# Layer norms of a network's first block: the features centred early on the mean of their first half, the variance corrected at the end

## The chip, the cores and the metric

The kernel runs on one core of one Trainium2 chip. The metric is the time of one execution on the device in microseconds (us), in fp32 accuracy, with all weights read from HBM. Five engines work beside one another, each in its own order: PE multiplies matrices, DVE and ACT work on rows of elements (DVE with two inputs, ACT with a function per element, for some of which it first loads a table), POOL has little to do here, and SP issues nearly all DMAs, in order, on one queue.

## The reference

The network has a first block of four layers (a gated convolution, a state space model "ssm", an rwkv mixer, a second convolution) and after it two blocks of attention and feed forward layers on two streams. The change concerns what closes each of the four layers:

```
for i in range(4):
    y = mixer_i(x)                                   # conv, ssm, rwkv, conv
    r = 8**0.25 * x + y
    r = r + (p[i] @ ple_proj[i]) * sigmoid(r @ ple_gate[i])
    mu = r.mean(-1); var = square(r - mu).mean(-1)
    x = (r - mu) * rsqrt(var + 1e-5) * ln_g[i] + ln_b[i]
```

`x` holds 256 tokens of 1024 features.

## The kernel before, in words

Features lie on partitions and tokens along the free axis, so `x` and `r` are 8 chunks (NCH) of 128 features by 256 tokens (S). A sum over features is then a matmul: the constant matrix `mean`, 128 x 128 with 1/1024 everywhere, times a chunk gives that chunk's part of the mean, the same on all partitions.

Weights come as fp32 tiles `w` of 128 x 1024 from HBM. Most are split into `whi` (ACT, L601) and `wlo` (DVE, L602), the operand likewise into `rs_hi`, `rs_lo`, and each product of 128 x 128 by 128 x 256 is three matmuls; a tile of `ple_gate` is 24 matmuls. The weights `ssm_in` are not split: their tile is 8 fp32 matmuls, straight from `w`. The sums `ps_st` are fp32 matmuls too. Each fp32 matmul leaves two records in the trace.

A stage of the first block ends in `finish`, which writes `r` and its split, and `ple_norm` follows. It runs `ple_proj` (its result is `pp`) and then the 8 tiles of `ple_gate`, one chunk m of the output per tile. For each, `take` runs: ACT a tanh out of PSUM (`ta<-ps_mm`), DVE `ta<-ta,pp`, DVE `r<-ta,r`, and for m = 1 to 6 DVE `total<-total,r`. After the last tile PE sums `total` and `r[7]` to the mean (`ps_st<-total`, `ps_st<-r`), DVE subtracts it from each chunk (`r<-r,ps_st`), ACT squares each (`sq<-r`), DVE adds up the squares (`sq<-sq`), PE sums them with three fp32 matmuls (`ps_st<-sq`). `rsqrt` is Ln, Exp and Square on ACT and two DVE steps, all under the name `tc`. Then DVE multiplies each chunk by `rstd` (`r<-r,pr,tc`, 8 of them) and ACT adds the bias (`x<-r,pr`); the next stage's matmuls read `x`. L403 and L433 are the lines of the helpers that record an operation of ACT or DVE, and a matmul.

The ssm stage that follows the first of the layer norms multiplies `x` by 16 tiles of `ssm_in` and treats the 8 chunks of its state one after another; chunk by chunk these are called A0, B1, A2, B3 up to B7 here, since two sets of buffers alternate. One chunk takes trigonometric functions on ACT, two wide multiplications, two additions, 8 scans and two more wide multiplications on DVE (`ssm_m`), then a sum on PE and `y`.

What fills gaps: from the start of the kernel a side generator `ada` makes the modulation vectors of the later blocks. It loads 512 KB tiles of `ada` through the same ring of four weight buffers `w` and the same SP queue, and DVE reduces each tile twice (`junk<-w,cond`, L1360). `Net.weave` steps it whenever the planned clock of the kernel has passed its due time and `hold` is zero; `ple_norm` raises `hold` when tile 6 of `ple_gate` has been taken and lowers it at its end. From the rwkv stage on the second stream's matmuls are woven in as well, which they are not before. The planner's model of the engines (`Model`, `Engine`, `TensorE`) with the pauses that a stage asks for (`yield 1.5`, `yield 3.5`) decides when a generator goes on; a scheduler behind it sets the order of the instructions on each engine.

Of the kernel before, what the change touches and what calls it, by code (L numbers as in the profile page):

```python
# [13 lines left out]
AF = mybir.ActivationFunctionType  # L14
ALU = mybir.AluOpType
# [3 lines left out]
D = 1024  # L19
S = 256  # L20
NCH = D // 128
# [65 lines left out]
def constants():  # L87
    groups = {}
    c = groups["base"] = Cols()
    c.add("ident", np.eye(128))  # L90
    c.add("mean", np.full((128, 128), 1.0 / D))
    c = groups["ssm"] = Cols()
    c.add("tshift", np.broadcast_to(np.arange(S // 2) - S // 4, (128, S // 2)))
    c.add("bd32", np.kron(np.eye(4), np.ones((32, 32))))
    c = groups["base"]
    bd = np.kron(np.eye(2), np.ones((64, 64)))
    c.add("bdmean", bd / 64)
    c = groups["rwkv"] = Cols()

    s_, t_ = np.arange(64)[:, None], np.arange(64)[None, :]  # L100
    strict, incl = (s_ < t_) * 1.0, (s_ <= t_) * 1.0
    c.add("p1mask", np.block([[strict, incl], [strict, incl]]))
    two = lambda m: np.kron(np.eye(2), m)
    c.add("ltmask", two(strict.T))
    c.add("eye", np.tile(np.eye(64), (2, 1)))
    for lv in range(6):
        b = 1 << lv
        m = (s_ // (2 * b) == t_ // (2 * b)) & (s_ // b % 2 == 0) & (t_ // b % 2 == 1)
        c.add(f"lv{lv}", np.tile(m * 1.0, (2, 1)))
    c.add("lvT0", two(((s_ == t_ + 1) & (s_ % 2 == 1)) * 1.0))  # L110
    c = groups["rwkv"]
    c.add("restart", np.broadcast_to((np.arange(S) % 64 != 0) * 1.0, (128, S)))
    c = groups["second"] = Cols()
    b96 = np.zeros((128, 128))
    b96[:96, :96] = 1.0 / 96
    c.add("b96", b96)
    ca, sa, ra = rope_head(64)
    cb, sb, rb = rope_head(32)
    c.add("cos_a", np.tile(ca.T, (2, 1)))
    c.add("sin_a", np.tile(sa.T, (2, 1)))  # L120
    c.add("rot_a", np.kron(np.eye(2), ra))
    full = lambda v, fill: np.concatenate([np.full((64, S), fill), v.T, np.full((32, S), fill)])
    c.add("cos_b", full(cb, 1.0))
    c.add("sin_b", full(sb, 0.0))
    r = np.zeros((128, 128))
    r[64:96, 64:96] = rb
    c.add("rot_b", r)
    t = np.arange(128)
    for lv in range(7):
        b = 1 << lv  # L130
        c.add(f"hg{lv}", (t[:, None] // (2 * b) == t[None, :] // (2 * b)) & (t[:, None] // b != t[None, :] // b))
    return groups


def rope_head(dim):

    f32 = np.float32
    t = np.arange(S)

    def one(pos, d):  # L140
        inv = np.power(f32(10000.0), -np.arange(0, d, 2, dtype=f32) / f32(d)).astype(f32)
        ang = pos.astype(f32)[:, None] * inv[None, :]
        ang = np.concatenate([ang, ang], axis=-1)
        return np.cos(ang), np.sin(ang)

    cr, sr = one(t // 64, dim // 2)
    cc, sc = one(t % 64, dim // 2)
    q = dim // 4
    m = np.zeros((dim, dim))
    for h in range(2):  # L150
        for i in range(q):
            a, b = h * 2 * q + i, h * 2 * q + q + i
            m[b, a], m[a, b] = -1.0, 1.0
    return np.concatenate([cr, cc], -1), np.concatenate([sr, sc], -1), m


def pack(inp):
# [97 lines left out]
    for g, c in constants().items():  # L255
        o["const_" + g] = c.array()
        cat.update({n: (g, k) for n, k in c.at.items()})
# [182 lines left out]
class Net:  # L440
# [339 lines left out]
    def ple_norm(self, R, i, split=True, free=2):  # L780

        nc = self.nc
        r, rs = R
        pp = yield from self.ple_proj(i)
        total = self.slot(free, [S], "total")

        def take(m, ps):
            t = self.tmp("ta")
            self.act(t, ps, AF.Tanh, scale=0.5)
            self.V.scalar_tensor_tensor(out=t, in0=t, scalar=1.0, in1=pp[:, m], op0=ALU.add, op1=ALU.mult)  # L790
            self.V.scalar_tensor_tensor(out=r[:, m], in0=t, scalar=0.5, in1=r[:, m], op0=ALU.mult, op1=ALU.add)
            if m == NCH - 2:
                self.hold += 1
            if 0 < m < NCH - 1:
                self.V.tensor_tensor(out=total, in0=total if m > 1 else r[:, 0], in1=r[:, m], op=ALU.add)

        yield from self.linear(f"ple_gate{i}", rs or r, take)
        yield 1.5
        mean = self.bsum(self.c("mean"), lambda k: (total, r[:, NCH - 1])[k], 2)
        sq = self.slot(2, [NCH, S], "sq")  # L800
        for k in range(NCH):
            self.V.tensor_tensor(out=r[:, k], in0=r[:, k], in1=mean, op=ALU.subtract)
            self.A.activation(out=sq[:, k], in_=r[:, k], func=AF.Square)
            if k > 2:
                self.V.tensor_tensor(out=sq[:, 0], in0=sq[:, 0], in1=sq[:, k - 2], op=ALU.add)
        yield 3.5
        var = self.bsum(self.c("mean"), lambda k: sq[:, (0, NCH - 2, NCH - 1)[k]], 3)
        rstd = self.rsqrt(var, 1e-5)
        x = self.xp.tile([128, NCH, S], F32, name="x")
        xs = self.pair(0, 1, "xs") if split else None  # L810
        for k in range(NCH):
            self.V.scalar_tensor_tensor(out=r[:, k], in0=r[:, k], scalar=self.p("ln_g", i * NCH + k), in1=rstd, op0=ALU.mult, op1=ALU.mult)
            self.A.activation(out=x[:, k], in_=r[:, k], func=AF.Identity, bias=self.p("ln_b", i * NCH + k))
            if split:
                self.split(x[:, k], xs[0][:, k], xs[1][:, k])
        self.hold -= 1
        yield 6.0
        return x, xs
# [1134 lines left out]
```

## Time and profile before

| what | value |
|---|---|
| time, median of 3 runs | 2898.12 us |
| lowest, highest | 2895.41, 2901.14 us |
| the profiled execution, its own time | 2892.28 us |
| its span | 2890.5 us |
| busy: PE, DVE, ACT | 2749.0, 2129.7, 1613.4 us |

The span is the time from the first to the last record on the core; 1.8 us of the profiled execution lie around it. The four layer norms follow one another at about 175, 396, 846 and 1020 us of the span, and the ssm stage takes the time from 195 to 323 us. A row of a timeline gives start, length, engine, line, operation, output and inputs; "x4" is four instructions in a row, and the bracket at its end says how long the engine was idle before and which engine's result ended that.

### The profile page before, as it was taken

The numbers are of one execution on the slowest core, as the hardware profiler recorded it, in microseconds if no ns is written. First come the engines' busy times: TensorE is split into PE (matmuls) and PEld (weight loads), VectorE is DVE, ScalarE is ACT, GpSimd is POOL, SyncE is SP. The second block draws the span as 40 slices with busy tenths as digits, with TensorE's granted clock in tenths as the row PEclk, the third lists the DMA queues.
The fourth block names the chain that finished last, engine by engine and source line by source line (L and its number), as shares of the span: only waits on it lengthen the run. The fifth ranks groups of instructions, "written<-read, shape, count | busy, mean of one in ns | idle before, by whom it ended". The sixth has DMA issues, their size and how long they took to land.

```text
span 2890.5 us, 58487 instructions
## 1 busy us (share of the span) xinstructions
PE 2749.0 (95%) x23798; PEld 2601.8 (90%) x23798; DVE 2129.7 (74%) x3950; ACT 1613.4 (56%) x2982; POOL 14.8 (1%) x41
## 2 busy tenths in 40 slices
PE   8978879899999999999999999999999999999999
PEld 8967779678999999898998978999999999996999
DVE  8868977566778798898899887877854336676655
ACT  5543657666664465877576766545423234466443
POOL 0000000000000000000000000000000000000000
PEclk9989889999999999999999999999999999999999
DMA  7643536001557657565575644666534223222554
GB/s 270 207 143 113 172 102 192 14 24 64 195 168 240 223 181 236 185 215 183 193 236 160 198 146 148 216 223 202 179 128 139 92 82 98 88 88 65 162 182 140
DMA packets 129295, 454.94 MB, mean 157 GB/s; under 512 B 14336, under 2 KB 18688, under 8 KB 128384
## 3 DMA queue, kind: packets, MB, share of 16 engines
q1 hardware_dynamic: 129024, 451.19, 48.3%
q8 instruction: 187, 3.06, 0.4%
q14 instruction: 84, 0.69, 0.1%
HBM read 450.09 MB, written 1.05 MB: 156 GB/s over the span
## 4 chain that ended last, share of the span: by engine, by line
PE 72%; DVE 13%; ACT 7%; DMA 5%; issue 3%; SPq 0%; ACTq 0%; DVEq 0%
PE ps_mm L433 62%; PE ps_ca L433 5%; DMA w<-in_ada_dram 4%; DVE wlo L602 3%; DVE junk L1360 3%; PE ps_cb L433 2%; DVE ssm_m L403 2%; ACT whi L601 2%; PE ps_st L433 2%; DVE tc L403 1%; PE ps_cb L437 1%; ACT L403 1%; ACT rw_b L403 1%; ACT tc L403 1%; DVE h_lo L403 1%
## 5 line engine op out<-in xcount | busy, mean ns | idle before, releaser
L601 ACT ACTIVATE whi<-w 128x1024 fp32r<-128x1024 f32 (+1 forms) x687 | 715.6, 1043 | 736.3 <-PE ps_mm L433 489.6
L602 DVE TENSOR_TENSOR wlo<-w,whi 128x1024 fp32r<-128x1024 f32 (+1 forms) x687 | 824.5, 1202 | 239.6 <-ACT whi L601 237.6
L433 PE MATMUL ps_mm<-h_hi,whi 128*128 128x256 f32 x3024 | 867.9, 289 | 6.4 <-ACT h_hi L403 4.8
L433 PE MATMUL ps_mm<-h_lo,whi 128*128 128x256 f32 x3024 | 856.5, 284 | 2.0 <-DVE h_lo L403 1.9
L433 PE MATMUL ps_mm<-h_hi,wlo 128*128 128x256 f32 x3024 | 853.0, 283 | 2.4 <-DVE wlo L602 2.4
L433 PEld LDWEIGHTS ps_mm<-h_hi,whi 128*128 128x128 f32 x3024 | 570.1, 189 | 15.8 <-ACT h_hi L403 6.5
L433 PEld LDWEIGHTS ps_mm<-h_lo,whi 128*128 128x128 f32 x3024 | 569.8, 189 | 8.3 <-DVE h_lo L403 3.2
L433 PEld LDWEIGHTS ps_mm<-h_hi,wlo 128*128 128x128 f32 x3024 | 571.2, 189 | 6.4 <-DVE wlo L602 4.0
L1360 DVE SCALAR_TENSOR_TENSOR junk<-w,cond 128x1024 bf16<-128x1024 f32 x288 | 351.0, 1219 | 123.9 <-DMA w<-in_ada_dram 122.8
L433 PE MATMUL ps_mm<-d_hi,whi 128*128 128x256 f32 x1232 | 352.9, 287 | 0.9 <-ACT d_hi L403 0.9
L433 PE MATMUL ps_mm<-d_hi,wlo 128*128 128x256 f32 x1232 | 348.5, 283 | 3.7 <-DVE wlo L602 3.6
L433 PE MATMUL ps_mm<-d_lo,whi 128*128 128x256 f32 x1232 | 349.9, 284 | 0.0
L433 PEld LDWEIGHTS ps_mm<-d_hi,wlo 128*128 128x128 f32 x1232 | 233.2, 189 | 4.9 <-DVE wlo L602 4.7
L433 PEld LDWEIGHTS ps_mm<-d_hi,whi 128*128 128x128 f32 x1232 | 232.6, 189 | 3.6 <-issue 2.0
L433 PEld LDWEIGHTS ps_mm<-d_lo,whi 128*128 128x128 f32 x1232 | 232.1, 188 | 2.7 <-issue 1.6
L403 DVE TENSOR_TENSOR td<-td,ps_mm 128x256 f32<-128x256 f32 x154 | 64.1, 416 | 82.5 <-PE ps_mm L433 79.1
L403 ACT ACT_TABLE_LOAD x84 | 107.8, 1283 | 2.5 <-PEq L1944 0.7
L403 ACT ACTIVATE d_hi<-td 128x256 fp32r<-128x256 f32 x154 | 63.0, 409 | 74.5 <-DVE td L403 73.8
L433 PE MATMUL ps_mm<-x_hi,whi 128*128 128x256 f32 x256 | 73.3, 287 | 11.8 <-ACT whi L601 11.8
L403 ACT ACTIVATE tc<-tc 128x256 f32<-128x256 f32 x182 | 75.1, 413 | 5.6 <-DVE tc L403 2.8
L403 ACT ACTIVATE td<-ps_mm 128x256 f32<-128x256 f32 x154 | 57.1, 372 | 33.1 <-PE ps_mm L433 32.6
L433 PE MATMUL ps_mm<-xs_hi,whi 128*128 128x256 f32 x256 | 72.7, 284 | 1.6 <-ACT whi L601 1.6
(465 smaller groups left out, 5287.9 us busy)
## 6 DMA issues: line engine op xcount, KB each, us to landing
w<-in_ffn_in_dram SPq DMA_DIRECT2D x268, 512.0 KB, 4.1
w<-in_ada_dram SPq DMA_DIRECT2D x144, 512.0 KB, 4.4
w<-in_ffn_out_dram SPq DMA_DIRECT2D x96, 512.0 KB, 4.0
w<-in_conv_in_dram SPq DMA_DIRECT2D x64, 512.0 KB, 4.6
w<-in_ffn_out_dram SPq DMA_DIRECT2D x48, 384.0 KB, 3.5
w<-in_ab_in_dram SPq DMA_DIRECT2D x34, 512.0 KB, 4.4
w<-in_ple_gate_dram SPq DMA_DIRECT2D x32, 512.0 KB, 4.4
w<-in_conv_out_dram SPq DMA_DIRECT2D x16, 512.0 KB, 4.7
```

The source lines that it names most:

```text
L403: return f(**kw)
L433: self.t.matmul(out, lhsT=lhsT, rhs=rhs, start=start, stop=stop)
L437: self.t.transpose(out, in_, ident)
L601: nc.scalar.activation(out=hi[:, :n], in_=w[:, :n], func=AF.Copy)
L602: nc.vector.tensor_tensor(out=lo[:, :n], in0=w[:, :n], in1=hi[:, :n].bitcast(F32), op=ALU.subtract)
L1360: nc.vector.scalar_tensor_tensor(out=self.junk, in0=w, scalar=1.0, in1=cb[:, s], op0=ALU.mult, op1=ALU.mult, accum_out=m[:, t, s:s + 1])
```

## The change

A constant `mean4`, 2/1024 everywhere, joins `mean`. `total` becomes a temporary `te` and adds only the chunks 0 to 3. As soon as chunk 4 is taken, one matmul of `mean4` with it gives c, the mean of the first half (`ps_ca<-te`). Chunks are then centred on c (`r<-r,ps_ca`), squared and added up while the tiles 5 to 7 are still multiplied. At the end four matmuls sum the centred chunks 4 to 7, whose result is the mean that remains, and two sum the squares; DVE takes the square of the remaining mean from the variance (`te<-ps_st,te`) and subtracts the remaining mean from all eight chunks (`r<-r,ps_st`) before they are multiplied by `rstd`. `hold` rises when chunk 4 is taken, the pause after the tiles is 1.0 and the second pause is gone. In the third layer norm the squares lie in another slot than before.

```diff
@@ -89,6 +89,7 @@
     c = groups["base"] = Cols()
     c.add("ident", np.eye(128))
     c.add("mean", np.full((128, 128), 1.0 / D))
+    c.add("mean4", np.full((128, 128), 2.0 / D))
     c = groups["ssm"] = Cols()
     c.add("tshift", np.broadcast_to(np.arange(S // 2) - S // 4, (128, S // 2)))
     c.add("bd32", np.kron(np.eye(4), np.ones((32, 32))))
@@ -782,30 +783,52 @@
         nc = self.nc
         r, rs = R
         pp = yield from self.ple_proj(i)
-        total = self.slot(free, [S], "total")
+        V, A, T = self.V, self.A, self.T
+        tt = lambda o, a, b, op: V.tensor_tensor(out=o, in0=a, in1=b, op=op)
+
+
+        H = NCH // 2
+        ss = self.slot(free, [NCH, S], "sq")
+        total = self.tmp("te")
+        st = {}
+
+        def centre(k):
+            tt(r[:, k], r[:, k], st["c"], ALU.subtract)
+            A.activation(out=ss[:, k], in_=r[:, k], func=AF.Square)
+            if 0 < k < NCH - 1:
+                tt(ss[:, 0], ss[:, 0], ss[:, k], ALU.add)
 
         def take(m, ps):
             t = self.tmp("ta")
             self.act(t, ps, AF.Tanh, scale=0.5)
-            self.V.scalar_tensor_tensor(out=t, in0=t, scalar=1.0, in1=pp[:, m], op0=ALU.add, op1=ALU.mult)
-            self.V.scalar_tensor_tensor(out=r[:, m], in0=t, scalar=0.5, in1=r[:, m], op0=ALU.mult, op1=ALU.add)
-            if m == NCH - 2:
+            V.scalar_tensor_tensor(out=t, in0=t, scalar=1.0, in1=pp[:, m], op0=ALU.add, op1=ALU.mult)
+            V.scalar_tensor_tensor(out=r[:, m], in0=t, scalar=0.5, in1=r[:, m], op0=ALU.mult, op1=ALU.add)
+            if m == H:
                 self.hold += 1
-            if 0 < m < NCH - 1:
-                self.V.tensor_tensor(out=total, in0=total if m > 1 else r[:, 0], in1=r[:, m], op=ALU.add)
+            if 0 < m < H:
+                tt(total, total if m > 1 else r[:, 0], r[:, m], ALU.add)
+            if m == H:
+                st["c"] = self.ps("ca")[:, :S]
+                T.matmul(st["c"], lhsT=self.c("mean4"), rhs=total, start=True, stop=True)
+                for k in range(3):
+                    centre(k)
+            elif m > H:
+                for k in ((), (3, 4), (5,), (6,))[m - H] if m < NCH - 1 else (6, 7):
+                    centre(k)
 
         yield from self.linear(f"ple_gate{i}", rs or r, take)
-        yield 1.5
-        mean = self.bsum(self.c("mean"), lambda k: (total, r[:, NCH - 1])[k], 2)
-        sq = self.slot(2, [NCH, S], "sq")
+        yield 1.0
+        ps = self.ps("st")
+        mean, var = ps[:, :S], ps[:, S:]
+        for k in range(H, NCH):
+            T.matmul(mean, lhsT=self.c("mean"), rhs=r[:, k], start=k == H, stop=k == NCH - 1)
+        for k in (0, NCH - 1):
+            T.matmul(var, lhsT=self.c("mean"), rhs=ss[:, k], start=k == 0, stop=k > 0)
+        A.activation(out=total, in_=mean, func=AF.Square)
+        tt(total, var, total, ALU.subtract)
+        rstd = self.rsqrt(total, 1e-5)
         for k in range(NCH):
-            self.V.tensor_tensor(out=r[:, k], in0=r[:, k], in1=mean, op=ALU.subtract)
-            self.A.activation(out=sq[:, k], in_=r[:, k], func=AF.Square)
-            if k > 2:
-                self.V.tensor_tensor(out=sq[:, 0], in0=sq[:, 0], in1=sq[:, k - 2], op=ALU.add)
-        yield 3.5
-        var = self.bsum(self.c("mean"), lambda k: sq[:, (0, NCH - 2, NCH - 1)[k]], 3)
-        rstd = self.rsqrt(var, 1e-5)
+            tt(r[:, k], r[:, k], mean, ALU.subtract)
         x = self.xp.tile([128, NCH, S], F32, name="x")
         xs = self.pair(0, 1, "xs") if split else None
         for k in range(NCH):
```

DVE in the middle of the first layer norm. Before, from the result of chunk 4 on, with `ada`'s reductions between:

```order
L403 TENSOR_TENSOR total<-total,r 128x256
L403 SCALAR_TENSOR_TENSOR r<-ta,r 128x256
L1360 SCALAR_TENSOR_TENSOR junk,mod<-w,cond_157 128x1024
L403 TENSOR_TENSOR total<-total,r 128x256
L1360 SCALAR_TENSOR_TENSOR junk,mod<-w,cond_157 128x1024
L403 SCALAR_TENSOR_TENSOR ta<-ta,pp 128x256
L1360 SCALAR_TENSOR_TENSOR junk,mod<-w,cond_157 128x1024
L403 SCALAR_TENSOR_TENSOR r<-ta,r 128x256
L1360 SCALAR_TENSOR_TENSOR junk,mod<-w,cond_157 128x1024
```

And after the change:

```order
L404 TENSOR_TENSOR te<-te,r 128x256
L404 SCALAR_TENSOR_TENSOR r<-ta,r 128x256
L1383 SCALAR_TENSOR_TENSOR junk,mod<-w,cond_157 128x1024
L404 TENSOR_TENSOR r<-r,ps_ca 128x256 x3
L404 SCALAR_TENSOR_TENSOR ta<-ta,pp 128x256
L404 TENSOR_TENSOR sq<-sq 128x256
L404 SCALAR_TENSOR_TENSOR r<-ta,r 128x256
L404 TENSOR_TENSOR sq<-sq 128x256
L404 TENSOR_TENSOR r<-r,ps_ca 128x256 x3
L404 TENSOR_TENSOR sq<-sq 128x256
L404 SCALAR_TENSOR_TENSOR ta<-ta,pp 128x256
```

In place of `ada`'s reductions and `total` there stand subtractions of c and sums of squares. The matmul that makes c stands in PE's order behind 14 of the 24 matmuls of tile 5 and waits for `te` of chunk 3, the row ahead of the last `r` here.

PE and DVE from the end of the first layer norm to the start of the ssm stage. PE before:

```order
L433 MATMUL ps_mm<-rs_hi,wlo 128x256
L433 MATMUL ps_st<-total,cs_base 128x256
L433 MATMUL ps_st<-r,cs_base 128x256
L433 MATMUL ps_st<-sq,cs_base 128x256 x3
L433 MATMUL ps_mm<-x,w 128x256 x24
L433 MATMUL ps_ca<-ta,bT_206 128x128
```

PE after:

```order
L434 MATMUL ps_mm<-rs_hi,wlo 128x256
L434 MATMUL ps_st<-r,cs_base 128x256 x4
L434 MATMUL ps_st<-sq,cs_base 128x256 x2
L434 MATMUL ps_mm<-x,w 128x256 x12
L434 MATMUL ps_ca<-ta,bT_206 128x128
```

The sums ask for four matmuls of `r` and two of `sq` in place of one of `total`, one of `r` and three of `sq`, and the first group of the ssm state (`ps_ca<-ta`) stands behind 12 matmuls with `x`, no longer behind 24. DVE before:

```order
L403 SCALAR_TENSOR_TENSOR ssm_m_2152<-ssm_m_2152 128x512
L1360 SCALAR_TENSOR_TENSOR junk,mod<-w,cond_157 128x1024 x3
L403 SCALAR_TENSOR_TENSOR tc<-ps_st,tc 128x256
L1360 SCALAR_TENSOR_TENSOR junk,mod<-w,cond_157 128x1024
L403 SCALAR_TENSOR_TENSOR tc<-tc 128x256
L1360 SCALAR_TENSOR_TENSOR junk,mod<-w,cond_157 128x1024
L403 SCALAR_TENSOR_TENSOR r<-r,pr,tc 128x256 x8
L403 TENSOR_TENSOR ssm_m_2152<-ssm_m_2153 128x1024 x2
L403 TENSOR_TENSOR ssm_m_2153<-ssm_m_2152 128x4x128 x2
L403 SCALAR_TENSOR_TENSOR ssm_m_2153<-rho,ssm_m_2153 128x128 x8
L403 TENSOR_TENSOR ssm_m_2152<-ssm_m_2153 128x1024 x2
L403 TENSOR_TENSOR ssm_m_2154<-ssm_m_2155 128x1024 x2
```

DVE after:

```order
L404 TENSOR_TENSOR te<-ps_st,te 128x256
L404 TENSOR_TENSOR r<-r,ps_st 128x256 x8
L1383 SCALAR_TENSOR_TENSOR junk,mod<-w,cond_157 128x1024
L404 SCALAR_TENSOR_TENSOR tc<-te,tc 128x256
L404 SCALAR_TENSOR_TENSOR tc<-tc 128x256
L404 SCALAR_TENSOR_TENSOR r<-r,pr,tc 128x256 x8
L1383 SCALAR_TENSOR_TENSOR junk,mod<-w,cond_157 128x1024 x2
L404 TENSOR_TENSOR ssm_m_2158<-ssm_m_2159 128x1024 x2
L404 TENSOR_TENSOR ssm_m_2159<-ssm_m_2158 128x4x128 x2
L404 SCALAR_TENSOR_TENSOR ssm_m_2159<-rho,ssm_m_2159 128x128 x8
L404 TENSOR_TENSOR ssm_m_2158<-ssm_m_2159 128x1024 x2
L404 SCALAR_TENSOR_TENSOR y<-u,pr,ps_st 128x2x128
```

Fewer reductions of `ada` stand between the steps of `rsqrt`, and two of them stand ahead of the first multiplication of A0. After A0 the chain goes on to `y`; before, B1's multiplications followed, so that the ssm stage had four rounds of two chunks, (A0,B1) to (A6,B7), and now has A0 alone, three pairs (B1,A2), (B3,A4), (B5,A6), and B7 alone.

SP's queue at the same place, before (the names carry their buffers' numbers):

```order
L596 DMA w_2156<-in_ssm_in_dram 128x1024
L1357 DMA w_2168<-in_ada0_dram 128x1024
L1357 DMA w_2172<-in_ada0_dram 128x1024
L596 DMA w_2176<-in_ssm_in_dram 128x1024
L1357 DMA w_2199<-in_ada0_dram 128x1024
L596 DMA w_2203<-in_ssm_in_dram 128x1024
```

And after:

```order
L1380 DMA w_2174<-in_ada0_dram 128x1024
L1380 DMA w_2178<-in_ada0_dram 128x1024
L597 DMA w_2182<-in_ssm_in_dram 128x1024
L597 DMA w_2243<-in_ssm_in_dram 128x1024
L597 DMA w_2266<-in_ssm_in_dram 128x1024
L775 DMA te_3715<-in_pT_dram 128x256
L1380 DMA w_2278<-in_ada0_dram 128x1024
L597 DMA w_2282<-in_ssm_in_dram 128x1024
L597 DMA w_2381<-in_ssm_in_dram 128x1024
```

`w_2278` is the `ada` tile of the two reductions ahead of A0. Its transfer waits for PE, that is, until the first tile of `ssm_in` (`w_2162`, before `w_2156`) has been multiplied and its buffer is free; the `ada` tiles at this place before (`w_2168` to `w_2226`) wait for DVE alone.

## Rows read from the trace of the kernel before

**Rows 1.** The page's part 1: busy time of each engine, its share, its instructions

```profile
PE 2749.0 (95%) x23798; PEld 2601.8 (90%) x23798; DVE 2129.7 (74%) x3950; ACT 1613.4 (56%) x2982; POOL 14.8 (1%) x41
```

**Rows 2.** Windows over three layer norms: stretch, its length, busy time by engine, PEclk, DMA

```profile
168.00:196.00 28.00, 8.35 (x33) 6.08 (x32) 22.92 (x51) 16.28 (x29) 0.00 (x0) 0.59 0.34 104
392.00:425.00 33.00, 20.76 (x112) 17.32 (x110) 25.67 (x72) 17.76 (x39) 0.00 (x0) 0.69 0.15 48
...
1016.00:1046.00 30.00, 30.00 (x244) 29.57 (x242) 26.20 (x53) 23.84 (x49) 0.00 (x0) 1.00 0.46 153
```

**Rows 3.** Timeline of PE, first layer norm: start, length, engine, line, operation, idle before

```profile
181.37 2.93 PE L433 MATMUL ps_st<-sq,cs_base 128*128 128x256 f32 x6 [4.50 <-DVE sq L403]
195.11 11.16 PE L433 MATMUL ps_mm<-x,w 128*128 128x256 f32 x39 [10.80 <-ACT x L403]
```

**Rows 4.** Timeline of DVE, first layer norm

```profile
165.58 0.41 DVE L403 TENSOR_TENSOR total<-total,r 128x256 f32<-128x256 f32 x1
...
166.25 1.22 DVE L1360 SCALAR_TENSOR_TENSOR junk<-w,cond 128x1024 bf16<-128x1024 f32 x1
...
174.99 1.22 DVE L1360 SCALAR_TENSOR_TENSOR junk<-w,cond 128x1024 bf16<-128x1024 f32 x1
...
191.07 0.42 DVE L403 SCALAR_TENSOR_TENSOR tc<-ps_st,tc 128x256 f32<-128x256 f32 x1 [4.33 <-ACT tc L403]
...
194.03 3.25 DVE L403 SCALAR_TENSOR_TENSOR r<-r,pr,tc 128x256 f32<-128x256 f32 x8
```

**Rows 5.** Timeline of ACT, first layer norm

```profile
161.85 0.39 ACT L403 ACTIVATE ta<-ps_mm 128x256 f32<-128x256 f32 x1 [1.67 <-PE ps_mm L433]
164.73 0.39 ACT L403 ACTIVATE ta<-ps_mm 128x256 f32<-128x256 f32 x1 [2.49 <-PE ps_mm L433]
...
181.45 1.28 ACT L394 ACT_TABLE_LOAD   x1
```

**Rows 6.** Timeline of DVE, ssm stage

```profile
210.58 3.69 DVE L403 TENSOR_TENSOR ssm_m<-ssm_m 128x1024 f32<-128x1024 f32 x4 [13.29 <-ACT ssm_m L403]
...
226.39 2.35 DVE L403 TENSOR_TENSOR ssm_m<-ssm_m 128x1024 f32<-128x1024 f32 x2
...
238.87 3.69 DVE L403 TENSOR_TENSOR ssm_m<-ssm_m 128x1024 f32<-128x1024 f32 x4 [2.45 <-ACT ssm_m L403]
...
266.67 3.69 DVE L403 TENSOR_TENSOR ssm_m<-ssm_m 128x1024 f32<-128x1024 f32 x4 [3.47 <-ACT ssm_m L403]
...
297.29 2.36 DVE L403 TENSOR_TENSOR ssm_m<-ssm_m 128x1024 f32<-128x1024 f32 x2
...
322.55 0.42 DVE L403 TENSOR_TENSOR ys_lo<-y,ys_hi 128x256 fp32r<-128x256 f32 x1
```

**Rows 7.** Timeline of PE, fourth layer norm

```profile
1020.60 0.60 PE L433 MATMUL ps_st<-total,cs_base 128*128 128x256 f32 x2
1021.03 0.68 PE L433 MATMUL ps_st<-r,cs_base 128*128 128x256 f32 x2
```

**Rows 8.** Timeline of ACT, start of the ssm stage

```profile
201.34 0.38 ACT L403 ACTIVATE u<-ps_mm 128x256 f32<-128x256 f32 x1 [3.50 <-PE ps_mm L433]
...
209.33 0.38 ACT L403 ACTIVATE ssm_m<-ps_ca 128x256 f32<-128x256 f32 x1 [0.23 <-PE ps_cb L433]
```

**Rows 9.** The page's part 6: DMA issues of the ada tiles, us to landing

```profile
w<-in_ada_dram SPq DMA_DIRECT2D x144, 512.0 KB, 4.4
```

**Rows 10.** Timeline of ACT, end of the second layer norm's tiles

```profile
395.93 0.37 ACT L403 ACTIVATE ta<-ps_mm 128x256 f32<-128x256 f32 x1
```

**Rows 11.** Timeline of DVE, second layer norm

```profile
409.15 3.26 DVE L403 SCALAR_TENSOR_TENSOR r<-r,pr,tc 128x256 f32<-128x256 f32 x8
```

**Rows 12.** Timeline of PE, a pause in the ssm stage

```profile
257.48 0.43 PE L433 MATMUL ps_st<-ta,ssm_s 128*32 128x128 f32 x8 [2.82 <-DVE y L403]
```

**Rows 13.** Windows behind that pause, columns as in rows 2

```profile
257.00:261.00 4.00, 3.52 (x73) 3.14 (x73) 3.93 (x8) 2.91 (x7) 0.00 (x0) 0.65 0.20 39
261.00:266.00 5.00, 5.00 (x48) 3.99 (x48) 1.79 (x4) 4.15 (x11) 0.00 (x0) 0.94 0.79 229
```

## The prediction

> **What bounds the kernel now.** First the page: PE is busy for 95% of the span [rows 1], so time can be won only where PE waits, and anything PE gets to do in addition is paid in full elsewhere. Next the windows over the layer norms [rows 2], which show two kinds. Around the first PE works 8.35 of 28 us at a mean clock of 0.59, around the second 20.8 of 33 us at 0.69. Around the fourth it works all 30 us at 1.00, because the second stream's matmuls fill it, and the third reads likewise. So the change can win in the first two norms, LN1 and LN2, and can only pay in LN3 and LN4.
>
> PE's own rows say what it waits for in LN1 [rows 3]: 4.50 us for the squares, then 10.80 us for `x`. The timelines of DVE and ACT [rows 4, 5] fill this in. The last row ahead of the mean is a reduction of `ada` at 174.99. Subtractions, squares and their sum take until 181.3. ACT then runs from 181.45 through five table loads and as many functions to 191.0 (the DVE row at 191.07 waited 4.33 us for it), and two more `ada` reductions delay the multiplication by `rstd` to 194.03. PE comes back at 195.11. The next bound lies in the ssm stage [rows 6]: it is DVE's and ACT's. Its rounds of two chunks start at 210.58, 238.87, 266.67 and 297.29, and what PE, DVE or ACT do between LN1 and the first round matters only as far as it moves that first start, the length of the rounds and the last row at 322.55.
>
> **The change, LN1.** The middle (eight subtractions, eight squares, sums) moves under the tiles 5 to 7. Its cover is the time of those tiles, 2.88 us each (164.73 less 161.85 on ACT [rows 5]), in which DVE now runs subtractions and sums in place of four `ada` reductions of 1.22 us [rows 4], so it has the room: a subtraction takes 0.41 and the next follows 0.33 later. The matmul for c is new and stands behind 14 matmuls of tile 5, at 161.8 + 14 x 0.12 = 163.5. It needs the sum of chunks 0 to 3, which ends at 165.58 + 0.41 = 165.99. PE pauses for 2.5 us, with 58 matmuls of the tiles queued behind. No row shows what this costs at the end; it lies between 0 (DVE ran behind PE by that much anyway: chunk 7 came out of DVE at 175.0, right ahead of the row at 174.99, and PE's last tile ended at 164.73 + 2 x 2.88 = 170.5) and 2.5. I take 0, since DVE's backlog is the nearer row: chunk 7 is ready at 175.0 again. One `ada` reduction stands ahead of its subtraction: 175.0 + 1.22 + 0.41 = 176.6. The last of the four mean matmuls and the two for the variance take 0.98 us each (six records in 2.93 us [rows 3]): 177.6 and 179.6. ACT squares the mean and starts its chain of 9.6 us at 178.1, not at 181.45, and ends at 187.7. The variance's correction and eight subtractions (0.4 + 8 x 0.33 = 3.1) lie beside that chain. The 2.96 us from 191.07 to 194.03 held two steps of 0.34 and two `ada` reductions of 1.14; the reductions are gone, so the multiplication starts at 187.7 + 0.7 and a hand-over, 188.5, rather than at 194.03: **5.5 us earlier**.
>
> **The ssm stage** gives part of it back. The first round waited for ACT's copy of the state's input out of PSUM at 209.33 [rows 8], and that for 24 matmuls with `x`; now it is 12. At 0.43 us each (1021.03 less 1020.60 [rows 7]) that is 5.2 us, and A0 could start at 210.58 - 5.5 - 5.2 = 199.9. But two reductions of `w_2278` stand ahead of it on DVE. SP issues that tile when the first tile of `ssm_in` has been used, 201.34 - 5.5 = 195.8 [rows 8]; with 4.4 us to land [rows 9] and 2 x 1.22 on DVE A0 starts at 202.6. On SP the load of `pT` stands ahead of it and waits until `te` is free, at about 188; that is before 195.8, so it costs nothing, and would cost what LN1 runs late beyond that. Then come five rounds, not four. A pair keeps DVE from 210.58 to 228.74, 9.1 us per chunk, and the next pair starts 10.1 us after that [rows 6]; A0 alone lies between 9.1 + 5 and 9.1 + 10.1, and I take 16, nearer to the lower end, because only one chunk's functions follow: 218.6. The pairs took 28.3, 27.8 and 30.6; two at 27.9 and one at 29.1 lead to 303.5. The last pair took 322.97 - 297.29 = 25.7; without one chunk's 9.1 and one `ada` reduction, 15.5: **319.0, 4.0 us earlier** than before.
>
> **LN2.** It has no `ada` reductions. The tanh of the last chunk starts at 395.93 [rows 10] and ends at 396.3; two DVE steps and a subtraction ahead of them 397.4, a `wlo` 398.5, a sum and the centring 399.2, one mean matmul and two for the variance at 0.98 each 402.2, the correction 402.6, six subtractions 404.6, and two steps of `rsqrt` mixed with two subtractions 406.2; ACT's functions lie beside these. With 0.35 for the hand-overs the multiplication starts at 406.55, and before it was 409.15 [rows 11]: **2.6 us earlier**. Bounds: 0 if PE's pause for c in tile 5 recurs here, 4.5 if the subtractions were hidden.
>
> **LN3 and LN4.** Seven fp32 matmuls in place of five on a full PE: 2 x 0.43 x 2 = **1.7 us more** [rows 7]. DVE's seven more steps, 7 x 0.34 = 2.4 us, fit beside, since DVE is busy 26.2 of 30 us [rows 2].
>
> **The clock.** After a pause of 2.82 us in the ssm stage [rows 12] PE's granted clock, which knows two levels, 1.2 and 2.4 GHz, is 0.65 of the higher one over 4 us and 0.94 over 5 us [rows 13]; that loses 4 x 0.35 + 5 x 0.06 = 1.7 us. The new pause is 2.5 us; at one chance in three this adds 0.6.
>
> The Trainium skill, "TensorE: Matmul & The Clock Gate", "HAM oscillation", speaks against this change: a PE that idles between its bursts falls back to the low rate, and each burst then starts at half speed. The rows agree so far as a pause goes; how far the low level would reach into tiles 5 to 7 no row shows, and by the page the sum would be that of the third rival.
>
> **Sum:** -4.0 - 2.6 + 1.7 + 0.6 = -4.3. The order of the second stream's matmuls after LN3 changes too, but PE is full there [rows 2]; I count it 0, plus or minus 2.9, the half spread of the three runs. The profiled execution took 2892.28, which gives 2888.0; the median is 5.8 higher, and I shift it likewise: **2893.8**.
>
> **Rivals.** (1) *The regrouping is free:* A0 starts at 199.9, because the tile lands in time, and the five rounds last no longer than four. For it: the stage does the same work. Against it: the wait for PE on SP. -10.7 - 2.6 + 1.7 = -11.6, 2886.5.
> (2) *The regrouping costs more than LN1 wins, slower.* Place: the ssm stage. B7's functions are now mixed with the stage's Gelu, so ACT loads five tables there where one was. If the three pair rounds take 30.6 as the third did, 3 x 2.7 = 8.1, and the five loads lie open at 1.28 each [rows 5], 6.4, the stage ends 14.5 later than forecast, 10.5 later than before: +10.5 - 2.6 + 1.7 = +9.6, 2907.7. It decides once the stage ends more than 6.7 us later than before. Against it: ACT is busy for 56% only [rows 1].
> The Trainium skill, "ScalarE: Activation LUTs", "What ACT_TABLE_LOAD costs", gives about 2.66 us for a switch, a drain included. The chain in LN1 [rows 4, 5] holds five loads and five functions in 9.6 us, less than five such switches; by the page this rival would be 6.9 us worse, and the measured load decides.
> (3) *PE's pause for c halves the clock over tiles 5 to 7.* 58 matmuls at 0.24 instead of 0.12 are 7.0 us, more than LN1's gain; the stage ends 3.0 later than before: +3.0 - 2.6 + 1.7 = +2.1, 2900.2. For it: the drop behind a pause of 2.82 us [rows 12, 13]. Against it: that drop was over within the first of the 5 us that follow.
>
> **How the numbers follow.** A difference of 0.2%, 5.8 us, is about what a measurement of this kernel can tell from none. The forecast gets 0.45 (of it 0.10 beyond -5.8, 0.34 within, 0.01 slower), rival 1 0.28 (faster), rival 2 0.12 (slower), rival 3 0.15 (0.13 within, 0.02 slower). So faster 0.38, same 0.47, slower 0.15. The range goes from 2885, just below rival 1, to 2902, above rival 3, and leaves rival 2 out, with some of rival 1's lower part.
>
> **What the new profile would show.** PE idle from 163.5 to 166 in tile 5, with its granted clock there; the first table load of LN1 at about 178; the first fp32 matmul with `x` at 189.6; A0's first multiplication at 202.6 behind two `ada` reductions; rounds of 28 us; the last `ys_lo` at 319; LN2's multiplication 2.6 us nearer to its last tile; PE full in LN3 and LN4. I am wrong if A0 doesn't wait for `w_2278`, if a round is longer than 30 us, or if the clock stays low after the pause.

## The result, and the profile after

The changed kernel takes 2924.18 us (median of 4 runs, 2916.36 to 2925.73); the kernel before, run beside it, 2897.26. The ratio is 1.0094, with an interval from 1.0082 to 1.0107: **slower by 27 us**. The forecast was 2893.8, within a range from 2885 to 2902.

The page of the changed kernel, its part 1 and one group of part 5 (busy us, mean ns; then the idle time before):

```profile
PE 2762.5 (94%) x23814; PEld 2613.5 (89%) x23814; DVE 2137.9 (73%) x3978; ACT 1638.3 (56%) x3004; POOL 14.8 (1%) x41
...
L404 ACT ACT_TABLE_LOAD x100 | 128.3, 1283 | 2.8 <-PEq L1967 0.7
```

and the same group on the page of the kernel before:

```profile
L403 ACT ACT_TABLE_LOAD x84 | 107.8, 1283 | 2.5 <-PEq L1944 0.7
```

PE's share is 94%, against 95% in [rows 1], and PE's and DVE's busy times rose by 13.5 and 8 us. ACT has 25 us more to do, and 20.5 of them are this group of table loads: 100 where 84 were. With the loads placed by hand, which have a line of their own (L395, before L394; 35 where 33 were), there are 135 where 117 were.

The norms themselves look better. The windows over the first, second and fourth, columns as in [rows 2]:

```profile
168.00:196.00 28.00, 14.12 (x69) 12.04 (x69) 19.00 (x46) 18.08 (x34) 0.00 (x0) 0.74 0.20 61
392.00:425.00 33.00, 21.61 (x136) 19.15 (x136) 29.34 (x82) 19.22 (x44) 0.00 (x0) 0.84 0.18 52
...
1016.00:1046.00 30.00, 30.00 (x242) 29.69 (x242) 25.18 (x54) 20.81 (x40) 0.00 (x0) 1.00 0.46 136
```

In the first stretch PE works 14.1 us where it worked 8.35, and its granted clock is 0.74 instead of 0.59. In the fourth PE is full, as before.

So where did 33 us go (the profiled execution took 2925.42 us, that of before 2892.28)? The splits of the weights on DVE (`wlo`) have the same number, 687, in both kernels, so the start of the k-th one is a clock. Its start in other kernels, less its start in the kernel before, in us, each from one trace (a kernel whose order is that of before up to the fourth norm reads +3.3 at 838, so a single difference of 3 to 4 us says little):

| at, in the kernel before | in the network | changed | third and fourth norm only | loads tied | before, one preload out |
|---|---|---|---|---|---|
| 341 us | behind the ssm stage | +2.8 | -0.8 | +0.6 | +0.1 |
| 484 | in rwkv | -1.4 | -0.8 | -1.8 | -0.2 |
| 838 | ahead of the third norm | -1.6 | -0.6 | -5.8 | 0.0 |
| 1073 | behind the fourth norm | +10.6 | +4.4 | +0.1 | +0.7 |
| 1510 | attention, ahead of the keys | +9.6 | +6.1 | +1.7 | -0.5 |
| 1620 | keys done | +27.0 | +21.4 | -0.9 | +12.3 |
| 1775 | behind the attention | +32.1 | +29.0 | +4.8 | +15.5 |
| 2877 | end | +33.1 | +29.5 | +5.8 | +19.6 |

The first two norms are 1.6 us ahead by 838. Then 12 us go between the third norm and the fourth's end, and 22 us in the attention, 17 in its key stage (1510 to 1620 us) and 5 right behind it, 500 us after the last changed line has run. The windows of these two stretches, of the kernel before

```profile
840.00:1075.00 235.00, 229.91 (x1864) 227.37 (x1864) 197.43 (x336) 137.53 (x224) 1.45 (x6) 0.99 0.62 201
...
1500.00:1720.00 220.00, 213.10 (x1542) 191.22 (x1541) 192.33 (x385) 150.75 (x258) 0.00 (x0) 0.99 0.55 177
```

and of the changed one:

```profile
840.00:1075.00 235.00, 224.59 (x1790) 221.43 (x1789) 191.36 (x330) 128.18 (x211) 1.46 (x6) 0.98 0.62 200
...
1500.00:1720.00 220.00, 195.22 (x1407) 181.07 (x1406) 174.57 (x334) 162.00 (x249) 0.00 (x0) 0.96 0.53 170
```

From 1500 to 1720 us PE works 195.2 us instead of 213.1, and gets 1407 matmul records done instead of 1542. Its largest wait there, changed and before (waited for, us, times, longest):

```profile
PE ps_ca L434 <- DVE tb L404: 18.9, 11, 5.5
```

```profile
PE ps_ca L433 <- DVE tb L403: 2.7, 3, 2.3
```

DVE in its turn waits there for ACT's steps of `rsqrt`, in a row that the list of the kernel before doesn't have:

```profile
DVE tc L404 <- ACT tc L404: 14.9, 8, 3.1
```

ACT's timeline at the start of the key stage shows why. First before: a Silu (`td<-ps_mm`), one load, then Ln, Exp and Square of two norms (`tc`) one after another:

```profile
1545.05 0.37 ACT L403 ACTIVATE td<-ps_mm 128x256 f32<-128x256 f32 x1
1545.44 1.28 ACT L394 ACT_TABLE_LOAD   x1
1546.73 0.47 ACT L403 ACTIVATE tc<-ps_st,fixed 128x256 f32<-128x256 f32 x1
1547.24 0.87 ACT L403 ACTIVATE tc<-tc 128x256 f32<-128x256 f32 x2
1548.01 0.46 ACT L403 ACTIVATE tc<-ps_mm,fixed 128x256 f32<-128x256 f32 x1
...
1549.32 0.41 ACT L403 ACTIVATE tc<-tc 128x256 f32<-128x256 f32 x1
```

And the changed kernel:

```profile
1553.59 1.28 ACT L395 ACT_TABLE_LOAD   x1
1554.88 0.42 ACT L404 ACTIVATE d_hi<-td 128x256 fp32r<-128x256 f32 x1
1555.32 1.28 ACT L395 ACT_TABLE_LOAD   x1
1556.61 0.47 ACT L404 ACTIVATE tc<-ps_st,fixed 128x256 f32<-128x256 f32 x1
1557.10 1.28 ACT L404 ACT_TABLE_LOAD   x1
1558.40 0.39 ACT L404 ACTIVATE td<-ps_mm 128x256 f32<-128x256 f32 x1
1558.80 1.28 ACT L404 ACT_TABLE_LOAD   x1
1560.10 0.42 ACT L404 ACTIVATE tc<-tc 128x256 f32<-128x256 f32 x1
...
1561.15 1.28 ACT L404 ACT_TABLE_LOAD   x1
1562.44 0.48 ACT L404 ACTIVATE tc<-ps_mm,fixed 128x256 f32<-128x256 f32 x1
...
1563.88 1.28 ACT L404 ACT_TABLE_LOAD   x1
```

Here two loads of line L395 come ahead of the first Ln, the Silu comes behind them with a table of its own, and from then on each Ln and each Exp loads its table: 19 loads start between 1545 and 1622 us, 2 in the same stage before (1535 to 1592 us).

The code says how. One set of tables holds Ln and Exp together, and `act` loads it by hand, once, when it believes another set is there:

```
if func == AF.Ln and self.acts != "ln":
    self.tc.keep_in_program_order(self.A.preload_act_table_set("natural_log_exp_and_others"))
    self.acts = "ln"
```

`self.acts` follows the order in which the program is written. The load is tied only behind the ACT instruction written right ahead of it, so the scheduler may move a Silu, written earlier still, behind the load. The Silu then brings its own table, `act` still believes in "ln", and each Ln and Exp takes a single table until the next load by hand. That the planner's time for the Silu's matmul decides this, and that the new third and fourth norm together shift it, is read from the code and not shown by a run; which kernels have the loads, and what they cost, the runs below show.

### The profile page after: what moved, and what is told of

Its sections match the earlier page's. It is cut to its first block, busy times and chain, and to the rows that moved or that the text cites. A ratio compares the mean times of both kernels' runs of the same rounds, so it can differ in the third digit from the quotient of the medians.

```text
span 2923.6 us, 58550 instructions
## 1 busy us (share of the span) xinstructions
PE 2762.5 (94%) x23814; PEld 2613.5 (89%) x23814; DVE 2137.9 (73%) x3978; ACT 1638.3 (56%) x3004; POOL 14.8 (1%) x41
## 4 chain that ended last, share of the span: by engine, by line
PE 60%; DVE 17%; DMA 10%; ACT 8%; issue 5%; SPq 0%; DVEq 0%; ACTq 0%
PE ps_mm L434 50%; DMA w<-in_ada_dram 7%; DVE wlo L603 5%; PE ps_ca L434 5%; DVE junk L1383 4%; PE ps_cb L434 2%; DVE ssm_m L404 2%; ACT whi L602 2%; DVE tc L404 2%; PE ps_st L434 2%; ACT L404 1%; PE ps_cb L438 1%; ACT tc L404 1%; DVE h_lo L404 1%; ACT rw_b L404 1%
```

## Experiments

**Each norm alone.** The old form is kept beside the new one, and a line chooses by the norm's number; (0,) is the first norm, (1,), (2,) and (3,) are the others:

```diff
+    def ple_norm(self, R, i, split=True, free=2):
+        return (self.ple_norm_new if i in (0,) else self.ple_norm_old)(R, i, split, free)
```

> The new form in the first layer norm alone, the old form in the other three. The instruction order from the second layer norm on is that of the kernel before. Theory P (the loss lies in the order of the second stream's matmuls and of ACT's table loads after the third norm, not in the norms): the first norm ends 4 to 5 us earlier, the ssm stage gives all but 1 us of it back, its last part (the gate) up to 3 more: -1 to +3 us against before. Rival R (the regrouped ssm stage is the loss): +5 us or more. Rival Q (the norm's extra work on a full PE and DVE is the loss): -1 to +3, since PE is not full here.

> The new form in the second layer norm alone. Only the rows of that norm differ in order from before. Theory P and rivals Q and R alike: -3 to -6 us, what the changed kernel's trace shows between the last tile's start and the next stage. If it is 0, the gain in that trace was borrowed from the ssm stage ahead of it.

> The new form in the third layer norm alone. DVE's order differs from before in about a thousand rows, from the third norm to the middle of the attention blocks, but ACT's order has 112 table loads where before has 117 and the changed kernel 135. Theory P: the order after it is a new draw; without the extra table loads the time lies between -5 and +12 us of before, and the 1500 to 1700 us stretch doesn't lose 20 us. Rival Q: +3 to +8, all of it within the norm itself.

> The new form in the fourth layer norm alone. DVE's order differs from before in 95 rows around that norm and nowhere else. Theory P: +1 us (two more fp32 matmuls of 0.43 us), at most +2. Rival Q: +4 us or more, because seven more DVE steps and two more matmuls meet engines that are full.

| new form in | median, us | ratio to before | interval |
|---|---|---|---|
| first norm | 2893.33 | 0.9997 | 0.9989 to 1.0006 |
| second | 2891.65 | 0.9994 | 0.9985 to 1.0003 |
| third | 2892.96 | 0.9991 | 0.9981 to 1.0002 |
| fourth | 2897.47 | 1.0003 | 0.9992 to 1.0013 |

None moves the time beyond its interval, and the ratios add up to -0.15%, or -4 us. So no norm in its new form is slow by itself, which is against rivals Q and R of these runs, and 27 us don't come from a sum of their parts.

**Pairs and threes.** The same line with (2, 3) and with (0, 1, 2).

> The new form in the third and fourth layer norm, the old in the first two. ACT's order has 131 table loads, 18 of them more in the key stage, as in the changed kernel. Each of the two norms alone left the time within 3 us of before. Theory T: the pair alone brings the loss, +24 to +33 us. Rival S' (the sum of small things): the sum of the single ones, -3 to +3 us.

> The new form in the first three layer norms, the old in the fourth: 116 table loads, none of the cluster in the key stage. Theory T: the loss is gone, -2 to -8 us against before (the sum of the single ones is about -6). Rival S': as the changed kernel less what the fourth norm costs alone, 2920 or more.

The third and fourth norm together: 2921.66 us, ratio 1.0085 (1.0069 to 1.0101). The first three: 2897.27 us, ratio 1.0002 (0.9992 to 1.0013). The pair brings nearly the whole loss, 23 us of it in the attention by the table above (15 in the key stage, 8 right behind it); without the fourth norm it is gone. The gain of 2 to 8 us expected of the three didn't show. The table loads go with the loss: from 1500 to 1720 us there are 20 before, 19 with the third norm alone, 20 with the fourth alone, 19 with the first three, and 37 with the pair, 38 in the changed kernel.

**Loads tied.** The changed kernel, with the load by hand tied behind the last ACT instruction that used another set too (NO_SYNC stands for a dependency that fixes the order and waits for nothing):

```diff
-            self.tc.keep_in_program_order(self.A.preload_act_table_set("natural_log_exp_and_others"))
+            pre = self.A.preload_act_table_set("natural_log_exp_and_others")
+            self.tc.keep_in_program_order(pre)
+            if self.other is not None:
+                self.tc.add_manual_dep(pre.ins, self.other.name, NO_SYNC, reason="table")
...
+        i = self.A.activation(out=out, in_=in_, func=func, **kw)
+        if self.acts != "ln":
+            self.other = i.ins
+        return i
```

> The changed kernel, in which each preload of the table set for Ln and Exp is tied behind the last ACT instruction that used another set, so that the scheduler can't move it ahead of that one. 112 table loads stand in ACT's order instead of 135; PE's and DVE's order is the changed kernel's but for some fifty and eighty rows. Theory T (the extra loads between 1545 and 1620 us are what the attention's key stage loses): that stretch wins back 15 to 20 us, 2903 to 2910. Rival S (PE waits there because products or DVE steps are in another order, the loads being ACT's slack): 0 to 5 us won back, 2919 or more.

> The kernel before with the same tie of the preloads: 105 table loads instead of 117. It tells what the tie does by itself. Theory T: before has no cluster of loads on a chain that PE waits for, so 0 to -4 us, not -15.

It takes 2899.08 us, ratio to before 1.0009 (0.9997 to 1.0020): 25 us less than the changed kernel, more than the 15 to 20 expected. The groups of table loads from 1500 to 1720 us (count, busy us, mean ns), in the changed kernel:

```profile
L404 ACT ACT_TABLE_LOAD x28 | 35.9, 1283 | 0.5
...
L395 ACT ACT_TABLE_LOAD x10 | 12.8, 1283 | 0.2
```

and with the tie:

```profile
L404 ACT ACT_TABLE_LOAD x14 | 18.0, 1283 | 0.3
...
L395 ACT ACT_TABLE_LOAD x9 | 11.5, 1283 | 0.2
```

38 loads became 23, and the two stretches read:

```profile
840.00:1075.00 235.00, 224.62 (x1818) 221.04 (x1817) 198.23 (x343) 128.39 (x212) 1.45 (x6) 1.00 0.63 202
...
1500.00:1720.00 220.00, 207.34 (x1509) 186.36 (x1508) 190.61 (x377) 152.56 (x255) 0.00 (x0) 1.00 0.56 178
```

PE wins back 12.1 us of work in the key stretch, and by the clock of splits the 17 us lost between 1510 and 1620 are gone (-2.6). From 840 to 1075 PE's busy time stays as it was in the changed kernel (224.6), with its clock at 1.00 instead of 0.98.

The tie on the kernel before gives 2890.71 us, ratio 0.9982 (0.9971 to 0.9994): -5 us, a little more than the 0 to -4 expected, and not 25. In its trace this is won between 484 and 838 us, where it has 17 loads in place of 26, as the changed kernel has with the tie. So part of the 25 us was never part of the loss: with the tie in both, the changed kernel is still 8 us slower (2899.08 against 2890.71). About 19 of the 27 us went with the loads, and 8 stay. In the traces of the tied changed kernel they lie between 838 and 1073 us (+5.9) and between 1620 and 1775 (+5.7), where it has no more loads than the kernel before; their cause is not shown.

**The loads alone.** The kernel before, norms untouched, without the one load by hand at 1545 us (the 24th in the program):

```diff
-            self.tc.keep_in_program_order(self.A.preload_act_table_set("natural_log_exp_and_others"))
+            self.npre += 1
+            if self.npre != 24:
+                self.tc.keep_in_program_order(self.A.preload_act_table_set("natural_log_exp_and_others"))
```

> The kernel before, in which one preload of the table set for Ln and Exp is left out, the one at the start of the attention's key stage (at 1545 us): Ln and Exp then load a table each until the next preload, 132 rows of loads in ACT's order instead of 117, with the norms as they were. Theory T (these loads by themselves cost what the changed kernel lost): +17 to +25 us, all of it between 1545 and 1620 us. Rival S (the reordering of the second stream was the loss, the loads were only beside it): +5 us or less.

2912.61 us, ratio 1.0060 (1.0044 to 1.0075): +17 us. Its loads and its window from 1500 to 1720 us:

```profile
L403 ACT ACT_TABLE_LOAD x29 | 37.2, 1283 | 0.5
...
L394 ACT ACT_TABLE_LOAD x6 | 7.7, 1283 | 0.1
```

```profile
1500.00:1720.00 220.00, 202.91 (x1444) 183.09 (x1443) 181.18 (x359) 161.53 (x257) 0.00 (x0) 0.98 0.54 169
```

35 loads where the kernel before has 20 there, and PE works 202.9 us instead of 213.1. Up to 1510 us its trace keeps within 1 us of before at the marks of the table above, and up to 1660 us the other instructions on PE, DVE and ACT stand in the order of before. So what is lost from 1510 to 1620 us, 12.8 us, is the work of the loads alone: fifteen at 1.28 us are 19.2 us, and two thirds of that lie on the path. All of the loss had been expected there. The rest, 3.2 us up to 1775 and 4.1 behind it, falls where DVE's and PE's order differs as well, from 1687 us on, so it isn't shown to be the loads'.

**What beats both.** The new form in some norms, with the tie:

> The second layer norm in the new form, the others in the old, and the preloads tied as in the run with the tie on before. If the two gains add, -4.5 - 2 to -3: 2888 to 2889 us, and faster than both kernels. If the second norm's gain was a chance of the runs, as the tie alone, 2890.7.

> The first and the second layer norm in the new form, preloads tied. Theory: the first norm's 5 to 6 us are given back in the ssm stage (five rounds, five table loads instead of one), so no more than 1 us beside the run with the second norm alone: 2887 to 2889. If the first norm keeps its gain: 2884.

> The second and the third layer norm in the new form, preloads tied, 103 rows of table loads. The third norm by itself left the time within 3 us; with the tie it should stay there: 2886 to 2891. If the third norm's two fp32 matmuls and its reordering cost 5 us, as the stretch from 840 to 1075 us in the changed kernel did, 2893 or more.

| new form in, with the tie | median, us | ratio to before | interval |
|---|---|---|---|
| none | 2890.71 | 0.9982 | 0.9971 to 0.9994 |
| second | 2888.49 | 0.9976 | 0.9966 to 0.9987 |
| first, second | 2888.56 | 0.9977 | 0.9964 to 0.9990 |
| second, third | 2888.15 | 0.9975 | 0.9966 to 0.9983 |

All are faster than both kernels. The three with new norms can't be told from one another, nor surely from the tie alone. All three came as expected: the first norm's gain isn't kept (2884 if it were), and the third norm's new form doesn't cost the 5 us that its stretch in the changed kernel suggested (2893 or more).

## Why the prediction was wrong

**The step that failed is the last term of the sum:** the second stream's order after LN3 changes too, "but PE is full there", so "I count it 0, plus or minus 2.9". In the traced execution what lies behind 838 us came to +33 by the clock of splits (12.2 to the fourth norm's end and 22.5 in the attention, less the 1.7 that were priced for the matmuls). The new order brought 17 more table loads into the key stage, and the runs put 17 to 19 of the 27 us on the loads: 17 when 15 such loads are added to the kernel before (12.8 of it where nothing else differs), 19 when the kernels are compared with the tie in both. The other 4.4 us by which the traced execution missed lie ahead of the third norm: -6.0 were forecast there, the clock included, and 1.6 were won. A full PE says that PE is the bound as long as its operands come in time; it says nothing of an order in which they don't. And the range for that term was taken from the spread of the runs, which is the noise of one order and no measure of the difference between two. What would have told it was there: the order of ACT's instructions has 117 rows of table loads before and 135 after, with 17 more in one place, the key stage (4 more in the ssm stage, 3 fewer at the third norm). The prediction read that order in the ssm stage only, where it saw five loads in place of one and priced them at 1.28 each.

**None of the three rivals was it.** The second had the right cause, table loads that lie open on ACT, in the wrong place. (Its sum has a slip: three rounds of 30.6 are 6.9 longer than the forecast's 27.9, 27.9 and 29.1, not 8.1, so it stood at 2906.5; that changes nothing here.) The fourth norm's price of seven full matmuls isn't the loss: alone it costs 0.03%, within its interval.

**LN1 came out as worked out.** The rows that answer to [rows 3 to 5], PE first:

```profile
164.74 0.67 PE L434 MATMUL ps_ca<-te,cs_base 128*128 128x256 f32 x2 [2.02 <-DVE te L404]
...
190.60 8.43 PE L434 MATMUL ps_mm<-x,w 128*128 128x256 f32 x24 [12.09 <-ACT x L404]
```

PE waits 2.0 us for `te` in tile 5 (2.5 forecast), and comes back at 190.60 (189.6). The granted clock over the next two stretches of 5 us:

```profile
165.00:170.00 5.00, 5.00 (x30) 0.66 0.40 135
170.00:175.00 5.00, 5.00 (x39) 1.00 0.00 0
```

It fell to 0.66 of the higher level for 5 us and was back at 1.00: 1.7 us, the very price that was given one chance in three, and DVE's backlog took it up, for chunk 7 is ready at 175.4 (175.0). The Trainium skill, "TensorE: Matmul & The Clock Gate", "HAM oscillation", says that a PE idle between bursts starts the next one slow. The trace agrees so far as the low level followed a pause, here of 2.0 us. It ended while the tiles went on, so the third rival's 7.0 us didn't come. ACT's chain begins at

```profile
178.94 1.28 ACT L395 ACT_TABLE_LOAD   x1
```

178.94 (178.1), and DVE goes on:

```profile
189.52 3.26 DVE L404 SCALAR_TENSOR_TENSOR r<-r,pr,tc 128x256 f32<-128x256 f32 x8
200.84 1.23 DVE L1383 SCALAR_TENSOR_TENSOR junk<-w,cond 128x1024 bf16<-128x1024 f32 x1 [8.07 <-DMA w<-in_ada_dram]
...
203.26 3.69 DVE L404 TENSOR_TENSOR ssm_m<-ssm_m 128x1024 f32<-128x1024 f32 x4
...
218.46 3.69 DVE L404 TENSOR_TENSOR ssm_m<-ssm_m 128x1024 f32<-128x1024 f32 x4 [2.45 <-ACT ssm_m L404]
...
275.94 2.36 DVE L404 TENSOR_TENSOR ssm_m<-ssm_m 128x1024 f32<-128x1024 f32 x2 [1.79 <-ACT ssm_m L404]
...
306.52 2.36 DVE L404 TENSOR_TENSOR ssm_m<-ssm_m 128x1024 f32<-128x1024 f32 x2
...
321.55 0.42 DVE L404 TENSOR_TENSOR ys_lo<-y,ys_hi 128x256 fp32r<-128x256 f32 x1
```

The multiplication by `rstd` starts at 189.52, 4.5 us earlier than before (5.5 forecast).

**The ssm stage gave more back than forecast.** Same rows, beside [rows 6]: A0 waited 8.07 us for the `ada` tile and began at 203.26 (202.6 forecast), the first pair at 218.46 (218.6). But the second pair's round ended at 275.94 (274.4) and the third took 30.6 us (306.52 less 275.94), where 29.1 was taken; the last `ys_lo` ends at 321.97, 1.0 us earlier than before and not 4.0. That 1.0 is gone right behind the stage: the table above has the changed kernel at +2.8 at 341 us, and LN2's last tanh starts at 396.76, 0.8 later than in [rows 10]. With the first norm alone the whole program wins 1 us, with an interval from -3 to +2.

**LN2** starts its multiplication at

```profile
406.17 3.25 DVE L404 SCALAR_TENSOR_TENSOR r<-r,pr,tc 128x256 f32<-128x256 f32 x8
```

3.0 us earlier than in [rows 11], although its last tile came 0.8 later: 9.4 us behind the last tanh, where before had 13.2 and 10.6 was forecast. Alone it is worth 2 us (-4 to +1) at the end.

**Between LN3 and LN4** 1.7 us were forecast, and the changed kernel lost 12 by the clock of splits. Two fp32 matmuls per norm don't explain that. What its trace shows there is DVE behind an `ada` tile that lands late, and PE behind DVE:

```profile
921.01 1.23 DVE L1383 SCALAR_TENSOR_TENSOR junk<-w,cond 128x1024 bf16<-128x1024 f32 x1 [4.05 <-DMA w<-in_ada_dram]
```

```profile
922.63 0.39 PE L434 MATMUL ps_mm<-xs_hi,whi 128*128 128x256 f32 x1 [2.27 <-DVE tb L404]
```

From 840 to 1075 us PE's idle time, and with it the part of each 5 us that the granted clock lacked, comes to 7.0 us before and 14.4 in the changed kernel. With the tie it is 10.7, though from 760 to 1550 us the order of PE, DVE and ACT and the table loads are those of the changed kernel: the idle time is the same 10.4 us, and the clock's part is 0.3 in place of 4.0. By the clock of splits the stretch costs 12.2 us in the changed kernel, 5.9 with the tie and 5.0 with the third and fourth norm alone. So part of the 12 us changes from one trace to another without a change of order or loads there, and the cause of the rest stays open: no run here isolates it.

**The table load.** The Trainium skill, "ScalarE: Activation LUTs", "What ACT_TABLE_LOAD costs", gives 2.66 us per switch with a drain. The rows show 1.28 and the next function 0.01 us behind it (1553.59 + 1.28, then 1554.88), and 15 loads added to the kernel before cost 12.8 us in their own stage and 17 in all, 0.85 to 1.16 each. The measurement decides.

## What to carry to other kernels

When a change passes through a planner or a scheduler, count instructions by kind and by stage over the whole program in the built order, on every engine, before pricing the part that was edited; a rise in table loads on ACT is a price that can be read there. A table set loaded by hand needs a tie to whatever could displace it, not just to its neighbour in the source. And the time of an engine that is "full" can't be taken for unchanged when its order, or that of an engine that feeds it, is new.

## What was not expected of the hardware

Table loads on a chain that PE waits for cost two thirds of their 1.28 us or more, even where PE has a second stream to work on: 15 of them cost 12.8 us where they stand, 0.85 each, and 17 us over the whole program. And a pause of PE as short as 2.0 us was followed by a granted clock of 0.66 over 5 us.
